# A decoder block whose TensorE queue is written by hand in the mixers: weaving order, new delays, an earlier second attention

## The chip, the cores and the metric

The kernel runs on one core of one Trainium2 chip. The metric is the device time of one execution in microseconds (us). Three runs of the kernel before gave 2710.49 us in the median, from 2708.99 to 2712.02. A program on this core drives five engines that run side by side: TensorE (PE) multiplies matrices, VectorE (DVE) and ScalarE (ACT) work elementwise, GpSimd (POOL) does a few small things, and SyncE (SP) issues the transfers (DMA). Each engine works off its own queue in the order in which the program was built; an instruction whose operands are not there holds up everything behind it on that engine.

## What is computed

One layer of a decoder block over 2048 tokens of width 1024, all in float32. The reference, cut to its skeleton:

```python
h = modulate(rms_norm(x, g_pre_mix), shift_m, scale_m)
proj = h @ w_in                      # attn q|k|v, mLSTM q|k|v|o, i|f gates, branch gates A|B
y_a = sliding_window_attention(rope(q_a), rope(k_a), v_a, sinks)     # 8 heads, 2 kv heads, window 128
q_m, k_m = silu(causal_depthwise_conv(q_m, k_m))
h_m = mlstm_chunkwise(q_m, k_m, v_m, i_pre, f_pre)                   # 4 heads of 128
y_m = sigmoid(o_m) * head_layer_norm(h_m)
merged = sigmoid(g_a) * (y_a @ w_branch_attn) + sigmoid(g_m) * (y_m @ w_branch_mlstm)
x = x + gate_m * rms_norm(merged @ w_out, g_post_mix)
h2 = modulate(rms_norm(x, g_pre_ffn), shift_f, scale_f)
x = x + gate_f * rms_norm((silu(h2 @ w_gate) * (h2 @ w_up)) @ w_down, g_post_ffn)
```

Every large product is made of three TensorE products of a high and a low part of each operand (`mm3`), so that the rounding of one part is made good by the other.

## The kernel before

**Stages.** The sequence is cut into two superblocks of 1024 tokens, each of two blocks of 512 (b0 and b1), each of four tiles of 128. A superblock (line 736 on) goes through the mixers: first the attention's queries (q) and keys and values with the gates' pre-activations (kv) of b0, then the mLSTM values (`vm`) of b0, then kv, q and `vm` of b1, then fourteen pairs of the projections that both blocks share (`in_pair`, line 1168; products of seven parts each that stand for eight), then the two output products of each block (`outputs`). After both superblocks comes the feed-forward part (`phase2`), which the change does not touch.

**Weaving.** The large products are a list of parts that `run2` goes through one by one. Everything else is a *stream*: a generator that emits a few instructions and then yields a delay. A virtual clock `now` counts the TensorE time emitted so far (`mm`, line 204, adds 0.422 ns per column of a two-part product, at least 110 ns; `transpose`, line 209, adds 110 ns). After each few products `tick` runs the streams whose delay is over. So a stream's delay says how much TensorE work is to lie between one of its steps and the next. The streams are

- `hprep` (line 486): eight steps that transpose the normalised input of a block, scale it on ACT and take its low part on DVE; for b1 each pair of steps is followed by four subtractions (lines 534 to 537) that build the sums T1 to T4 for the shared products;
- `hsums` (line 540): a transfer within the on-chip memory and eight casts and subtractions (lines 551 and 552) that split two of these sums;
- `q_stream` and `k_stream` (lines 764 and 791): after the rotary embedding (`rope`, lines 757 to 761, on DVE), TensorE transposes, and the result is stored to DRAM;
- `gates` (line 832): the scans of the mLSTM gates;
- `attention` (line 895), two at a time (`attention_stream`, streams 0 and 1 take every other tile): load, 24 score products, maximum on DVE, exponentials on ACT (line 946), a product on POOL (line 950), 16 transposes, four products with the values (PV), evacuation and store;
- `mlstm`, with `chunk_state` and `chunk_out` for each of eight tiles, and `conv` for the convolution.

**What sets the order.** `build` opens the program with a scheduler that simulates the engines (`schedule_with_timeline_sim=True`): on each engine it places next what its simulation finds ready. So in the kernel before, the order in which the program emits instructions, and with it every delay, is only a proposal. On all five engines the queue is what the scheduler made of it.

**Pools.** PSUM has four banks for the large products (`acc`) and four for all streams (`mix`). Split weights have four tiles, raw weights two.

Of the kernel before, what the change touches and what calls it, by code (L numbers as in the profile page):

```python
# [24 lines left out]
NT = TB // P  # L25
# [3 lines left out]
T2 = 1024  # L29
# [6 lines left out]
NEG = -1.0e30  # L36


L_X, L_HT, L_HS = 16000.0, 1400.0, 1500.0
L_ROPE, L_ROPEK, L_QK, L_ATT2 = 5000.0, 2100.0, 1500.0, 3500.0  # L40
L_GATE, L_SCAN = 1800.0, 3000.0
L_SOFT, L_PT, L_PV = 8000.0, 1300.0, 1000.0
L_ML, L_KW, L_OUT, L_STATE = 3200.0, 2600.0, 1500.0, 1500.0
L_S, L_LN = 1800.0, 5000.0
L_LOAD, L_HP2, L_HC = 5000.0, 1000.0, 3000.0
L_TANH, L_CONV, L_HD = 1500.0, 4000.0, 5000.0
L_REST = (2000.0, 1800.0, 2500.0, 2500.0)

# [23 lines left out]
def decoder_block(ctx: ExitStack, tc: tile.TileContext, a: dict, out: bass.AP, dbg=None):  # L72
# [124 lines left out]
    now = [0.0]  # L197
# [13 lines left out]
    def spawn(gen, delay=0.0):  # L211
        st = [now[0] + delay, gen, False]
        streams.append(st)
        return st
# [15 lines left out]
    def finish(sts):  # L230
        for st in sts:
            while not st[2]:
                now[0] = max(now[0], min(q[0] for q in streams))
                tick()
# [251 lines left out]
    def hprep(b, first=False):  # L486

        odd = b % 2
        xs = []
        xbs = x_first if first else [load_x(x_d[b * TB:(b + 1) * TB, :], big, i) for i in range(2)]  # L490
        V_NAMES = ("T3", "T2") if odd else ("T1", "T4")
        for n in V_NAMES:
            HR[n] = big([4, TB])
        vs = [HR[n] for n in V_NAMES]
        for i in range(2):
            xb = xbs[i]
            ss = small.tile([P, 4], F32, tag="ss", name=nm("ss"), bufs=4)
            for t in range(2):
                for hf in range(2):
                    A.activation(vs[i][:, 2 * t + hf, :], xb[:, t, hf * 512:(hf + 1) * 512], AF.Square,  # L500
                                 accum_out=ss[:, 2 * hf + t:2 * hf + t + 1])
            V.tensor_tensor(ss[:, 0:2], ss[:, 0:2], ss[:, 2:4], op=ALU.add)
            r = rsqrt_of_sumsq(ss[:, 0:2], 2)
            for t in range(2):
                if first:
                    A.activation(xb[:, t, :], xb[:, t, :], AF.Copy, scale=r[:, t:t + 1])
                else:
                    V.tensor_scalar(xb[:, t, :], xb[:, t, :], r[:, t:t + 1], None, op0=ALU.mult)
                xs.append(xb[:, t, :])
        yield L_X  # L510

        def one(k):
            name = f"{k // 4 + 1}{odd + 1}"
            hi, lo = (hc_part(name, i)[:, k % 4, :] for i in range(2))
            ps = mix_tile()
            for t in range(NT):
                transpose(ps[:, t * P:(t + 1) * P], xs[t][:, k * P:(k + 1) * P])
            A.activation(hi, ps, AF.Identity, scale=s1[:, k:k + 1], bias=sh1[:, k:k + 1])  # L518
            v = vs[k // 4][:, k % 4, :]
            A.activation(v, ps, AF.Identity, scale=s1[:, k:k + 1], bias=sh1[:, k:k + 1])  # L520
            (G if first else V).tensor_tensor(lo, v, hi.bitcast(F32), op=ALU.subtract)

        if not odd:
            for k in range(KD):
                one(k)
                yield L_HT
            return
        for k in range(4):
            one(k)
            yield L_HT  # L530
            one(k + 4)
            yield L_HT
            t1, t2, t3, t4 = (HR[n][:, k, :] for n in ("T1", "T2", "T3", "T4"))
            V.tensor_tensor(t1, t3, t1, op=ALU.subtract)
            V.tensor_tensor(t3, t2, t3, op=ALU.subtract)
            V.tensor_tensor(t2, t2, t1, op=ALU.subtract)
            V.tensor_tensor(t4, t4, t2, op=ALU.subtract)
            yield L_HT

    def hsums(names):  # L540

# [194 lines left out]
    def superblock(sb):  # L736
# [158 lines left out]
        def attention(n):  # L895
# [71 lines left out]
            for src_, u, st_, sp_ in ((pfs, int(first), True, first), (pcs, 1, False, True)):  # L967
                for g, p_ in enumerate(src_):
                    mm(yps[g * 64:(g + 1) * 64, :], vat[:, u, g * 64:(g + 1) * 64], p_.rearrange("p j q -> p (j q)"), st_, sp_)
            now[0] -= 1500.0  # L970
            yh, yl = tm([P, 512], F32R), tm([P, 512], F32R)
            A.copy(yh, yps)
            V.tensor_tensor(yl, yps, yh.bitcast(F32), op=ALU.subtract)
# [5 lines left out]
        def attention_stream(u):  # L979
            for i in range(u, 2 * NT, 2):  # L980
                while i >= ready[0]:
                    yield 1000.0
                yield from attention(b0 * NT + i)
                done_att[0] += 1
                yield 500.0
# [1 line left out]
        done_att = [0]  # L987

        def attend(b):
            finish(R["qk"])  # L990
            ready[0] = (b - b0 + 1) * NT
            if b == b0:
                R["att"] = [spawn(attention_stream(0), L_QK), spawn(attention_stream(1), L_QK + L_ATT2)]
            R["gs", b] = [spawn(gates(b), L_QK)]

        def end_attention(n):
            while done_att[0] < n:
# [283 lines left out]
        yield start  # L1281
        for z in q_kv(b0):
            yield from z
        yield lambda: attend(b0)
        yield from vm(b0)
        yield lambda: finish([hps[b1]])
        yield lambda: hps.update(t=spawn(hsums(("T2", "T4"))))
        q1, kv1 = (list(z) for z in q_kv(b1))
        yield from kv1
        yield from q1  # L1290
        yield from vm(b1)

        def start_f():
            finish([hps["t"]])
            HC.pop("12")
            hps["t"] = spawn(hsums(("T1", "T3")))
            attend(b1)

        yield start_f
        pairs = [("om", 0), ("qk", 0), ("om", 1), ("qk", 1), ("ga", 0), ("qk", 2), ("ga", 1), ("qk", 3),  # L1300
# [1 line left out]
        for i, (kind, p) in enumerate(pairs):  # L1302
            parts = list(in_pair(kind, p))
            if sb == 0 and i == 4:
                yield lambda: R.update(ada_m=[spawn(ada_stream([(2, "gate")], 6000.0))])
            if i == 0:
                yield from parts[:3]
                yield lambda: finish([hps["t"]])
                parts = parts[3:]
            if i + 1 == len(pairs):  # L1310
                yield from parts[:2]
                yield lambda: end_attention(NT)
                yield lambda: (load_y(b0, 0), load_g(b0, 0))
                parts = parts[2:]
            yield from parts
            if (kind, p) == ("qk", 3):
                yield lambda: finish(convs + R["gs", b0] + R["gs", b1])
                yield lambda: spawn(mlstm(), L_ML)
# [4 lines left out]
    hps = {}  # L1323
# [485 lines left out]
    def open_ffn():  # L1809
        p1.close()  # L1810
        F["pool"] = ctx.enter_context(tc.tile_pool(name="fpool", bufs=1, reuse_waits="tile"))

    def program():
        for i, ch in enumerate(ADA):
            if i == 3:
                yield lambda: tables.update({0: rope_tables(0)})
            yield lambda ch=ch: first_h(*ch)
        items = [it for sb in range(NSB) for it in superblock(sb)]
        last = max(i for i, it in enumerate(items) if isinstance(it, Part))
        yield from items[:last]  # L1820
        yield lambda: next(phase2)
        yield from items[last:]

# [46 lines left out]
```

## Time and profile before

| | |
|---|---|
| runs, median (lowest to highest) | 2710.49 us (2708.99 to 2712.02) |
| the profiled execution | 2716.59 us |
| its span in the profile | 2714.9 us |
| mean granted TensorE clock | 0.99 |
| first superblock's mixers | about 50 to 683 us |
| second superblock's mixers | about 683 to 1420 us |
| feed-forward part | about 1420 to 2715 us |
| largest transfer groups | weights of the input projection, 48 of 1024 KB; 154 stores of 256 KB |

A profile shows one execution. Busy time of an engine is given per stretch of the span; the granted clock is the share of the full TensorE clock that the throttle let through; "idle before" an instruction is put down to what released it. Matmuls overlap: a product of 512 columns is listed with some 0.39 us, while in a dense stretch one starts every 0.23 us. So whether TensorE is held up is read from its idle time, its clock and the number of products in a stretch together.

### The profile page before, as it was taken

To read this page: it belongs to the slowest core of one execution; us is meant where nothing else is said; L and a number is where in the kernel's file an instruction comes from. 1 tells how busy PE (TensorE), PEld (TensorE's weight loads), DVE (VectorE), ACT (ScalarE), POOL (GpSimd) and SP (SyncE) were. 2 spreads that over 40 slices of the span, in tenths; PEclk is the share of its full clock that TensorE was granted. 3 is DMA by queue.
4 is the path that set the end of the run, shared out by engine and by line. 5 is a ranking of instruction groups with operands and counts; after the bars stand their busy time and mean duration, and the time that the engine had idled before them with its cause. 6 is when DMAs were issued, how large, how long until landed. Compare 5 with 4: busy or idle time off the path is not lost.

```text
span 2714.9 us, 35793 instructions
## 1 busy us (share of the span) xinstructions
PE 2639.2 (97%) x12310; PEld 2138.9 (79%) x12310; DVE 1986.2 (73%) x3906; ACT 1299.8 (48%) x2558; POOL 148.2 (5%) x189
## 2 busy tenths in 40 slices
PE   6989999999998999999999999999999999999998
PEld 4867788888885678888887888888877888888886
DVE  7968788778695778876687777776677676766456
ACT  5556544444755564444563443335554333333444
POOL 2010001100101000110000000000000000000000
PEclk8999999999998999999999999999999999999999
DMA  7654355897574544678765564436675232324566
GB/s 249 206 184 157 128 172 179 269 340 248 196 235 147 196 138 138 213 231 291 251 224 198 175 201 152 155 113 213 215 271 188 97 117 86 113 97 144 186 210 217
DMA packets 353639, 511.90 MB, mean 189 GB/s; under 512 B 25120, under 2 KB 213660, under 8 KB 348208
## 3 DMA queue, kind: packets, MB, share of 16 engines
q1 hardware_dynamic: 353456, 509.61, 56.9%
q8 instruction: 97, 1.59, 0.2%
q14 instruction: 86, 0.70, 0.1%
HBM read 357.12 MB, written 144.02 MB: 185 GB/s over the span
## 4 chain that ended last, share of the span: by engine, by line
PE 85%; DVE 7%; DMA 4%; ACT 2%; issue 1%; POOL 0%; SPq 0%; DVEq 0%; ACTq 0%; POOLq 0%
PE acc L204 61%; PE mix L204 22%; PE mix L209 2%; DVE hl L1357 1%; DVE tm L428 1%; DMA raw<-as_d 1%; ACT tm L946 1%; ACT hl L1356 1%; DMA raw<-in_w_in_dram 1%; DMA at_d<-tx 0%; DMA big<-in_x_dram 0%; DVE wlo L260 0%; DMA tx<-in_w_ada_dram 0%; DVE w L1667 0%; DMA at<-at_d 0%
## 5 line engine op out<-in xcount | busy, mean ns | idle before, releaser
L204 PE MATMUL acc<-big,hl 128*128 128x512 f32 x3936 | 940.8, 394 | 4.3 <-ACT tx L827 1.8
L204 PEld LDWEIGHTS acc<-big,hl 128*128 128x128 f32 x3936 | 733.3, 188 | 172.5 <-issue 13.8
L1356 ACT CAST hl<-raw 128x512 fp32r<-128x512 f32 x732 | 440.1, 621 | 493.4 <-PE acc L204 222.2
L1357 DVE TENSOR_TENSOR hl<-raw,hl 128x512 fp32r<-128x512 f32 x732 | 496.3, 694 | 194.8 <-ACT hl L1356 194.0
L204 PE MATMUL acc<-whi,big 128*128 128x512 f32 (+1 forms) x1280 | 379.3, 377 | 10.8 <-ACT big L518 8.4
L204 PEld LDWEIGHTS acc<-whi,big 128*128 128x128 f32 x1280 | 236.2, 192 | 52.4 <-ACT big L518 8.5
L204 PE MATMUL mix<-big,hl 128*128 128x512 f32 x1056 | 263.9, 391 | 1.7 <-ACT hl L1356 1.1
L204 PE MATMUL acc<-wlo,big 128*128 128x512 f32 (+1 forms) x640 | 241.2, 379 | 6.4 <-DVE wlo L260 6.4
L204 PE MATMUL acc<-hl,hl 128*128 128x512 f32 x1008 | 237.4, 393 | 5.1 <-DVE hl L1357 3.4
L204 PEld LDWEIGHTS mix<-big,hl 128*128 128x128 f32 x1056 | 197.9, 188 | 45.9 <-ACT hl L1356 1.9
L204 PEld LDWEIGHTS acc<-hl,hl 128*128 128x128 f32 x1008 | 187.0, 188 | 50.9 <-DVE hl L1357 8.8
L204 PE MATMUL mix<-hl,hl 128*128 128x512 f32 x792 | 182.7, 391 | 1.3 <-DVE hl L1357 0.9
L204 PEld LDWEIGHTS mix<-hl,hl 128*128 128x128 f32 x792 | 147.9, 188 | 35.3 <-DVE hl L1357 3.1
L204 PE MATMUL acc<-big,whi 128*128 128x512 f32 x512 | 157.4, 393 | 0.0
L260 DVE TENSOR_TENSOR wlo<-raw,whi 128x1024 fp32r<-128x1024 f32 (+1 forms) x96 | 109.0, 1137 | 65.5 <-ACT whi L259 59.8
L259 ACT CAST whi<-raw 128x1024 fp32r<-128x1024 f32 (+1 forms) x96 | 94.3, 983 | 123.8 <-PE acc L204 110.4
L204 PEld LDWEIGHTS acc<-wlo,big 128*128 128x128 f32 x640 | 123.7, 193 | 28.3 <-DVE wlo L260 8.6
L475 POOL TENSOR_TENSOR rs<-ms,nhalf 128x1 f32<-128x1 f32 (+1 forms) x56 | 42.6, 772 | 1617.5 <-DVE ms L473 1610.5
L204 PE MATMUL mix<-hcT4h,hl 128*128 128x512 f32 x352 | 117.7, 395 | 0.7 <-ACT hl L1356 0.7
L204 PE MATMUL acc<-hcT2h,hl 128*128 128x512 f32 x352 | 117.6, 394 | 0.0
L204 PEld LDWEIGHTS acc<-big,whi 128*128 128x128 f32 x512 | 95.4, 188 | 19.2
L204 PE MATMUL acc<-big,wlo 128*128 128x512 f32 x256 | 97.7, 393 | 0.0
(330 smaller groups left out, 3491.5 us busy)
## 6 DMA issues: line engine op xcount, KB each, us to landing
raw<-in_w_in_dram SPq DMA_DIRECT2D x48, 1024.0 KB
as_d<-w SPq DMA_DIRECT2D x154, 256.0 KB
raw<-as_d SPq DMA_DIRECT2D x70, 512.0 KB
raw<-in_w_ffn_gate_dram SPq DMA_DIRECT2D x22, 1024.0 KB
raw<-in_w_ffn_up_dram SPq DMA_DIRECT2D x22, 1024.0 KB
raw<-ws_d SPq DMA_DIRECT2D x40, 512.0 KB
y_d<-tm SPq DMA_DIRECT2D x64, 256.0 KB
tx<-in_w_ada_dram SPq DMA_DIRECT2D x64, 256.0 KB
```

The source lines that it names most:

```text
L204: T.matmul(o, lhsT=lhsT, rhs=rhs, start=start, stop=stop, skip_group_check=resumed)
L209: T.transpose(o, i, ident[:k, :k])
L259: A.copy(hv, src)
L260: V.tensor_tensor(lv, src, hv.bitcast(F32), op=ALU.subtract)
L428: V.scalar_tensor_tensor(acc, raw[:, k, :], c_, acc, op0=ALU.mult, op1=ALU.add)
L475: G.tensor_tensor(r[:, :n], ms[:, :n], nhalf[:, :n], op=ALU.pow)
L946: A.activation(sc[g][:, j, :], sc[g][:, j, :], AF.Exp, bias=nm_[:, hd:hd + 1], accum_out=sums[:, hd:hd + 1])
L1356: A.copy(v(hi), src)
L1357: V.tensor_tensor(v(lo), src, v(hi).bitcast(F32), op=ALU.subtract)
```

## The change

TensorE's queue is taken out of the scheduler's hands: from the end of the first q product of the first superblock up to the last part of the mixers, a manual schedule for PE alone makes TensorE issue in the order in which the program emits. DVE, ACT, POOL and SP are still scheduled by simulation. Beside that

- nearly all delays are set anew, most of them longer (`L_SOFT` between scores and the first transposes 8 to 12 us, `L_PV` 1 to 3 us, `L_QK` 1.5 to 6 us, `L_ROPE` 5 to 7 us, `L_ROPEK` 2.1 to 3 us, `L_LN` 5 to 9 us), and a correction of the virtual clock by 1.5 us in `attention` is taken out;
- the four subtractions per step of b1's `hprep` get a stream of their own, `hcombos`, which is started after `vm` of b0 with a delay of 12 us and goes on with the sums T2 and T4; T1 and T3 are split by two streams instead of one, T3 later;
- `attend`, which opens a block's gates and attention, no longer drains the q and k streams at its place: it starts a stream that looks every 0.3 us whether they are done, waits `L_QK`, and then lets the attention of that block begin; for b1 it is called ahead of `vm` instead of behind it;
- the second attention stream looks for work every 4.5 us instead of every 1 us.

```diff
-L_ROPE, L_ROPEK, L_QK, L_ATT2 = 5000.0, 2100.0, 1500.0, 3500.0
-L_GATE, L_SCAN = 1800.0, 3000.0
-L_SOFT, L_PT, L_PV = 8000.0, 1300.0, 1000.0
-L_ML, L_KW, L_OUT, L_STATE = 3200.0, 2600.0, 1500.0, 1500.0
-L_S, L_LN = 1800.0, 5000.0
-L_LOAD, L_HP2, L_HC = 5000.0, 1000.0, 3000.0
+L_X, L_HT, L_HS, L_HCB = 16000.0, 1400.0, 1500.0, 12000.0
+L_ROPE, L_ROPEK, L_QK, L_ATT2 = 7000.0, 3000.0, 6000.0, 7000.0
+L_GATE, L_SCAN = 6000.0, 9000.0
+L_SOFT, L_PT, L_PV = 12000.0, 1500.0, 3000.0
+L_ML, L_KW, L_OUT, L_STATE = 3200.0, 3500.0, 1500.0, 1500.0
+L_S, L_LN = 2500.0, 9000.0
+L_LOAD, L_HP2, L_HC = 7000.0, 1000.0, 3000.0
...
+    def hcombos():
+        for k in range(4):
             t1, t2, t3, t4 = (HR[n][:, k, :] for n in ("T1", "T2", "T3", "T4"))
             V.tensor_tensor(t1, t3, t1, op=ALU.subtract)
             V.tensor_tensor(t3, t2, t3, op=ALU.subtract)
+            yield L_HS
             V.tensor_tensor(t2, t2, t1, op=ALU.subtract)
             V.tensor_tensor(t4, t4, t2, op=ALU.subtract)
-            yield L_HT
+            yield L_HS
+        yield from hsums(("T2", "T4"))
...
-            now[0] -= 1500.0
...
                 while i >= ready[0]:
-                    yield 1000.0
+                    yield 1000.0 + 3500.0 * u
...
         def attend(b):
-            finish(R["qk"])
-            ready[0] = (b - b0 + 1) * NT
+            def stream():
+                while not all(st[2] for st in R["qk"]):
+                    yield 300.0
+                yield L_QK
+                ready[0] = (b - b0 + 1) * NT
+                yield from gates(b)
+            R["gs", b] = [spawn(stream())]
             if b == b0:
                 R["att"] = [spawn(attention_stream(0), L_QK), spawn(attention_stream(1), L_QK + L_ATT2)]
-            R["gs", b] = [spawn(gates(b), L_QK)]
...
         for z in q_kv(b0):
             yield from z
+            if sb == 0 and not pe_order:
+                pe_order.append(0)
+                yield lambda: order.enter_context(tc.manual_schedule(engines={mybir.EngineType.PE}))
...
-        yield lambda: hps.update(t=spawn(hsums(("T2", "T4"))))
+        yield lambda: hps.update(t=spawn(hcombos(), L_HCB))
...
         yield from q1
+        yield lambda: attend(b1)
         yield from vm(b1)
...
-            hps["t"] = spawn(hsums(("T1", "T3")))
-            attend(b1)
+            hps["t"] = spawn(hsums(("T1",)))
+            hps["t3"] = spawn(hsums(("T3",)), L_HD)
...
-                yield from parts[:3]
+                yield from parts[:4]
                 yield lambda: finish([hps["t"]])
-                parts = parts[3:]
+                yield parts[4]
+                yield lambda: finish([hps["t3"]])
+                parts = parts[5:]
...
         yield from items[:last]
+        yield order.close
         yield lambda: next(phase2)
```

No product, elementwise instruction or transfer is added or taken away: the same products, transposes, casts, subtractions and transfers are issued, in another order.

More of the change, by code (lines that the diff above doesn't have):

```diff
@@ L36 @@
 NEG = -1.0e30
-L_X, L_HT, L_HS = 16000.0, 1400.0, 1500.0
-L_ROPE, L_ROPEK, L_QK, L_ATT2 = 5000.0, 2100.0, 1500.0, 3500.0
-L_GATE, L_SCAN = 1800.0, 3000.0
-L_SOFT, L_PT, L_PV = 8000.0, 1300.0, 1000.0
-L_ML, L_KW, L_OUT, L_STATE = 3200.0, 2600.0, 1500.0, 1500.0
-L_S, L_LN = 1800.0, 5000.0
-L_LOAD, L_HP2, L_HC = 5000.0, 1000.0, 3000.0
+L_X, L_HT, L_HS, L_HCB = 16000.0, 1400.0, 1500.0, 12000.0
[5 more added lines that the diff above has]
+L_LOAD, L_HP2, L_HC = 7000.0, 1000.0, 3000.0
 L_TANH, L_CONV, L_HD = 1500.0, 4000.0, 5000.0
@@ L1811, in open_ffn @@
         F["pool"] = ctx.enter_context(tc.tile_pool(name="fpool", bufs=1, reuse_waits="tile"))
+    pe_order, order = [], ExitStack()
     def program():
```

## The prediction

> **What bounds the kernel now.** I read the page's busy times first, then the stretches, then the waits and the timeline of the stretches that stand out.
>
> ```profile
> span 2714.9 us, 35793 instructions
> ...
> PE 2639.2 (97%) x12310; PEld 2138.9 (79%) x12310; DVE 1986.2 (73%) x3906; ACT 1299.8 (48%) x2558; POOL 148.2 (5%) x189
> ```
>
> TensorE is the bound, but a busy TensorE is not a dense one. The stretches below (PE, weight loads, DVE, ACT, POOL busy, granted clock, DMA share, GB/s) show where it is thin.
>
> ```profile
> core 0: us, PE busy (x) PEld busy (x) DVE busy (x) ACT busy (x) POOL busy (x), PEclk, DMA share, GB/s
> 66.00:108.00 42.00, 39.46 (x242) 34.61 (x241) 39.77 (x105) 27.01 (x46) 1.17 (x2) 1.00 0.56 171
> 155.00:186.00 31.00, 24.14 (x116) 12.52 (x114) 16.13 (x44) 16.64 (x56) 4.68 (x5) 0.89 0.46 143
> 206.00:312.00 106.00, 105.97 (x504) 76.33 (x504) 83.57 (x182) 67.31 (x173) 9.36 (x8) 1.00 0.41 132
> 312.00:683.00 371.00, 371.00 (x1796) 311.64 (x1795) 293.00 (x622) 177.18 (x317) 32.14 (x32) 1.00 0.71 235
> 403.00:570.00 167.00, 167.00 (x889) 143.00 (x889) 127.96 (x323) 77.31 (x150) 25.36 (x22) 1.00 0.76 243
> 741.00:783.00 42.00, 39.13 (x239) 34.32 (x238) 37.13 (x104) 21.94 (x36) 0.00 (x0) 1.00 0.60 184
> 838.00:868.00 30.00, 20.58 (x95) 11.12 (x92) 15.03 (x42) 15.81 (x55) 4.67 (x5) 0.72 0.37 116
> 1750.00:1800.00 50.00, 50.00 (x220) 40.97 (x219) 39.33 (x64) 18.10 (x33) 0.00 (x0) 1.00 0.43 139
> ```
>
> The last row is the feed-forward part: 220 products of 512 columns in 50 us, 0.227 us each. That is dense. In the mixers two stretches are not: 155 to 186 us (6.9 us idle, clock 0.89) and 838 to 868 us (9.4 us idle, clock 0.72). They are the third and fourth attention tile of each superblock's first block. And in two stretches DVE is all but full: 39.77 of 42 us and 37.13 of 42. They are the fronts of the superblocks, where the rotary embedding of q and k, the low parts of b1's input and the sums T1 to T4 meet. All else that the change reorders (206 to 312, and 312 to 683 with the mLSTM tiles at 403 to 570) has next to no idle time on TensorE, so there it can only lose.
>
> **Part 1: what TensorE's new order takes out.** In 838 to 868 us TensorE waits in turn for loads, DVE and POOL:
>
> ```profile
> PE mix L209 <- DVE tm L933: 4.1, 1, 4.1
> PE mix L204 <- DMA at<-at_d: 2.4, 1, 2.4
> PE mix L209 <- POOL tm L950: 1.6, 2, 0.9
> ```
>
> The reason is in the queue: the old order puts 4.0 and 5.3 us of TensorE work between the last scores of these tiles and their first PV product, since the scheduler laid scores, transposes and PV of both tiles back to back. (I count TensorE work through the two queues with 0.227 us per product of 512 columns, 0.12 for 264, 0.105 for a transpose, 0.115 for a score product, 0.87 for a PV product.) The chain that has to fit in:
>
> ```profile
> 841.08 2.74 PE L204 MATMUL mix<-at 64*128 64x256 f32 x24 [2.43 <-DMA at<-at_d]
> 845.10 2.93 PE L204 MATMUL mix<-at 64*128 64x256 f32 x24 [1.28 <-DVE tm L933]
> 846.63 1.28 ACT L946 ACT_TABLE_LOAD   x1 [2.18 <-DVE es L941]
> 850.25 1.04 POOL L950 TENSOR_TENSOR tm<-tm,sums 128x512 f32<-128x512 f32 x1 [25.52 <-DVE sums L949]
> 854.26 4.37 PE L204 MATMUL mix<-tm,at 128*64 128x512 f32 x8
> 858.22 1.04 POOL L950 TENSOR_TENSOR tm<-tm,sums 128x512 f32<-128x512 f32 x1 [5.06 <-DVE sums L949]
> 861.49 1.68 PE L204 MATMUL mix<-tm,at 128*64 128x512 f32 x2
> ```
>
> From the end of the scores (843.8 and 848.0) to the end of the first POOL product (851.3 and 859.3) it takes 7.5 and 11.2 us, to PV 10.4 and 13.5. The new order has 11.5 to 13.2 us between scores and first transposes for the sixteen tiles, and 16.8 to 20.3 to PV. So products of `vm` and kv cover the chain, with 4 us to spare for the first tile of a pair and half a microsecond for the second. What can come back: idle 6.86 + 9.42 = 16.3 us, and some 4 us of slow clock, 20 at most. I take 16, since the second tile's chain is not quite covered.
>
> On the clock the Trainium skill has a rule ("TensorE: Matmul & The Clock Gate", "Why this matters for your kernels"): idle gaps over about 3 us drop TensorE to half its clock until it has been busy for as long again. The granted 0.72 and 0.89 agree. By it each long wait that the new order makes costs up to 2 us more than the wait; the sum below would be some 5 us higher.
>
> **Part 2: what it puts in: the rotary embeddings of the fronts.** Here TensorE's transposes move the other way. Between the last product of the first q tile and the transpose of the last k tile the old order has 38.6 and 39.2 us of TensorE work (first and second superblock), the new one 21.1 and 24.9: `L_ROPE` and `L_ROPEK` count from each evacuation, and the transposes now stand where the program emits them, in front of the products of `vm` that used to cover them. DVE can't keep up:
>
> ```profile
> 68.29 0.42 DVE L757 TENSOR_TENSOR tx<-tx,sin 128x256 f32<-128x256 f32 x1
> 102.66 0.22 DVE L761 TENSOR_TENSOR tx<-tx,tx 128x64 f32<-128x64 f32 x1
> ...
> 743.03 0.42 DVE L757 TENSOR_TENSOR tx<-tx,sin 128x256 f32<-128x256 f32 x1
> 743.36 0.42 DVE L758 TENSOR_TENSOR tx<-tx,sin 128x256 f32<-128x256 f32 x1
> ...
> 744.37 0.68 DVE L536 TENSOR_TENSOR big<-big,big 128x512 f32<-128x512 f32 x1
> 744.97 0.70 DVE L260 TENSOR_TENSOR wlo<-raw,whi 128x528 fp32r<-128x528 f32 x1
> 745.59 0.69 DVE L759 TENSOR_TENSOR tx<-tx,cos 128x512 f32<-128x512 f32 x1
> ...
> 760.08 1.22 DVE L260 TENSOR_TENSOR wlo<-raw,whi 128x1024 fp32r<-128x1024 f32 x1
> ...
> 777.52 0.22 DVE L761 TENSOR_TENSOR tx<-tx,tx 128x64 f32<-128x64 f32 x1
> ```
>
> From the first q rotation to the last k rotation DVE takes 34.6 us (68.29 to 102.88) and 34.7 (743.03 to 777.74). TensorE did not feel it, because it came to the last k transpose only at 107.7 and 782.3:
>
> ```profile
> 107.71 0.27 PE L209 MATMUL mix<-ident,tx 128*128 128x128 f32 x1
> ...
> 782.34 0.27 PE L209 MATMUL mix<-ident,tx 128*128 128x128 f32 x1
> ```
>
> In the changed kernel's DVE queue the same stretch in the second superblock holds 16 rotations of half a tile at 0.335 us (start to start above) and 4 at 0.60, 36 subtractions of 128x512 at 0.60 (8 low parts, 16 sums T, 8 low parts of T2 and T4 that the scheduler pulled forward, 4 low parts of q), 3 split weights at 0.62 and 2 at 1.22, and 6.4 us of small ones: 40 us. The delay of `hcombos` doesn't keep its subtractions out, since it orders TensorE's queue alone. In the first superblock the queue has 33.1 us. With 0.6 us for ACT's copy ahead of it, TensorE is late by 33.1 + 0.6 - 21.1 = 12.6 and 40.0 + 0.6 - 24.9 = 15.7 us, 28 together. Behind the waiting transposes stand all products of `vm`, ready as they are. The old queue lost 42 - 39.46 = 2.5 and 42 - 39.13 = 2.9 us there, so 23 are new. What DVE did early it need not do later: I take back 5 us, for the eight pulled-forward subtractions. Net 18. The bounds: 5 if the scheduler's queue runs better than its sum, 28 if nothing comes back.
>
> **Part 3: the second block's attention and the rest.** The four tiles of b1 lie within 62 us of TensorE work (scores of the first to PV of the last), against 106 us in the row 206 to 312. DVE's queue holds 47 us for these 62, but 21 for the first 17.5. So 3 us of wait in each superblock, from 0 (the convolutions give way) to 8. That `attend` for b1 stands ahead of `vm` moves the first score by 1 us of TensorE work only: it still waits for the q streams and `L_QK`. Eight mLSTM tiles take 97 us of TensorE work instead of 145, and DVE's queue 85 us in them (88%), where the row 403 to 570 shows 127.96 of 167 (77%). The shortest distance there is scores to numerator, 2.1 us:
>
> ```profile
> 433.67 1.06 PE L204 MATMUL mix<-ld,ld 128*128 128x128 f32 x8
> 435.87 0.69 DVE L1051 TENSOR_TENSOR tm<-mix,tm 128x512 f32<-128x512 f32 x1
> ```
>
> That chain ended 1.8 us after the scores, so it fits where DVE is free at once and is late by one instruction (0.7 us) where not: 2.5 us for eight tiles. The old queue also let two products slip ahead at many part boundaries of the pairs, the new one doesn't; a cast of one evacuation (0.6 us) lies under a part of 12 x 0.227 = 2.7 us, so nothing, at worst 0.5 us at some 60 places in both superblocks. Loads have 7 instead of 5 us and cost nothing.
>
> **The sum.** -16 + 18 + 2 x 3 + 2 x 2.5 = +13 us against the profiled execution's 2716.6. That one lies 6.1 us above the median of the runs, 2710.5, so the forecast is 2723.5, rounded 2723.
>
> **The rivals.** *The fronts are covered (faster).* If DVE's wait in the fronts is no longer than the 5 us of before plus 5, because TensorE's other work there (ACT, raw weights) was late anyway, and b1 costs nothing, the sum is -16 + 5 + 5 = -6 to -11: 2702. For it: DVE was full in both fronts before (39.77 and 37.13 of 42), and TensorE lost under 3 us. Against: it lost little because of the 14 to 17 us of cover that are now gone.
>
> *Pair boundaries decide (much slower).* TensorE stops at each boundary where the old queue slipped, 60 places at 0.5 us, once DVE is over 88% full: +30, 2750. For it: the 88%. Against: in 312 to 683 us nothing waited.
>
> *It evens out.* The change doesn't make TensorE denser, it moves the wait from the third and fourth tile to the rotation, at equal price (16 against 16): 2710 within 5 us. For it: DVE's work is the same and it is the engine that both wait for.
>
> **How the numbers follow.** A measurement tells 0.2% (5.4 us) from no change. Forecast 0.42 (own range 2712 to 2740), covered fronts 0.29, boundaries 0.14, even 0.15. Slower by over 0.2% (above 2715.9): most of the forecast, all of the boundaries, 0.53; same 0.15; faster (below 2705.1) 0.32. The range goes from 2688 (nearly all of 20 us gained, the fronts covered) to 2752.
>
> **What would show it.** Right: in the changed kernel TensorE waits for DVE's key rotation (transposes out of tx) in both fronts, over 10 us each; no waits for POOL over 2 us at the third and fourth tile; clock near 1.00 there. Part 2 falls if the idle time of the fronts stays near 3 us. Part 3 falls if idle time appears at the pairs. Wrong altogether would be a wait that none of these stretches held, such as a transfer that SP, still in the scheduler's order, issues too late for TensorE's fixed one.

## The result, and the profile after

The changed kernel is slower: 2792.72 us in the median (2787.18 to 2793.43), against 2711.24 us for the kernel before in the same comparison, a ratio of 1.0294 [1.0278, 1.0309]. The profiled execution took 2792.43 us. The forecast was 2723, with a range up to 2752: the sign was right, the size was not.

The page after, its span and its busy times:

```profile
span 2790.7 us, 35799 instructions
...
PE 2642.5 (95%) x12310; PEld 2150.0 (77%) x12310; DVE 1992.1 (71%) x3906; ACT 1306.1 (47%) x2558; POOL 152.0 (5%) x189
```

The span grew by 75.8 us, TensorE's busy time by only 3.3 (2639.2 before). So some 72 us are idle time of TensorE, and the stretches say where. Rows of the changed kernel (PE, weight loads, DVE, ACT, POOL busy, clock, DMA share, GB/s). Its second superblock runs 23 us late in the front (the first rotation starts at 766.36 us, before at 743.03), so the rows of the kernel before that belong to it, in the second fence, are taken 23 us earlier. Further on the lag grows, and the rows hold somewhat different work; since the kernel before has only 3.4 us of idle time from 892 us to the end of its mixers, the differences of idle time stand all the same:

```profile
66.00:108.00 42.00, 30.99 (x184) 27.35 (x183) 40.67 (x106) 26.50 (x47) 0.79 (x2) 0.88 0.54 176
130.00:186.00 56.00, 46.55 (x268) 35.52 (x269) 30.29 (x117) 34.62 (x113) 8.85 (x9) 0.88 0.52 158
206.00:312.00 106.00, 97.18 (x479) 72.14 (x478) 78.96 (x171) 65.94 (x170) 8.84 (x8) 0.95 0.45 153
403.00:570.00 167.00, 155.54 (x827) 131.05 (x826) 127.11 (x325) 75.52 (x153) 26.27 (x22) 0.99 0.64 201
764.00:812.00 48.00, 32.47 (x194) 29.29 (x193) 41.52 (x105) 26.66 (x46) 0.00 (x0) 0.82 0.58 193
812.00:915.00 103.00, 89.38 (x476) 68.95 (x476) 62.73 (x189) 48.78 (x140) 9.69 (x9) 0.89 0.50 157
915.00:1010.00 95.00, 77.71 (x403) 58.24 (x402) 69.09 (x150) 52.27 (x145) 9.55 (x8) 0.91 0.55 182
1080.00:1250.00 170.00, 155.92 (x782) 130.04 (x781) 135.97 (x321) 73.84 (x149) 23.96 (x20) 0.97 0.54 167
```

```profile
130.00:186.00 56.00, 49.15 (x227) 31.75 (x226) 33.09 (x101) 32.99 (x108) 9.38 (x9) 0.94 0.43 130
741.00:789.00 48.00, 44.96 (x282) 39.65 (x280) 41.28 (x113) 23.81 (x40) 0.00 (x0) 1.00 0.66 214
789.00:892.00 103.00, 89.45 (x462) 65.72 (x460) 74.20 (x204) 53.16 (x147) 9.20 (x9) 0.90 0.58 191
892.00:987.00 95.00, 91.60 (x435) 68.57 (x435) 73.85 (x166) 62.59 (x166) 8.32 (x8) 0.98 0.50 156
1057.00:1227.00 170.00, 170.00 (x889) 144.78 (x889) 138.25 (x330) 76.95 (x153) 26.84 (x22) 1.00 0.68 211
```

The first two columns after the stretch are its length and TensorE's busy time; the difference is its idle time. Put beside the terms of the forecast, that gives (us):

| term of the forecast | forecast | idle time, before to after | change |
|---|---|---|---|
| fronts with the rotary embeddings (part 2) | +23, net +18 | 2.5 to 11.0 and 3.0 to 15.5 | +21 |
| attention of b0, third and fourth tiles (part 1) | -16 | 6.9 to 9.5 and 13.6 to 13.6 | +3 |
| attention of b1 (part 3) | +6 | 0.0 to 8.8 and 3.4 to 17.3 | +23 |
| mLSTM (part 3) | +5 | 0 to 11.5 and 0 to 14.1 | +26 |

What TensorE waited for in the mixers (us in total, times, longest):

```profile
PE mix L209 <- DVE tx L766: 24.0, 8, 5.4
PE mix L204 <- issue: 14.2, 4, 5.9
PE acc L204 <- ACT tx L832: 12.0, 3, 8.0
PE mix L204 <- DVE tm L938: 9.6, 5, 3.1
PE acc L204 <- ACT tx L1511: 7.0, 2, 4.1
PE mix L204 <- DVE tm L857: 6.7, 2, 4.3
PE mix L204 <- DVE tm L1027: 5.0, 5, 2.0
```

Only the first line was in the forecast with a size near this (L766 is the last step of the rotation, line 761 before; line numbers are those of the changed kernel from here on). The second and the last belong together: the state products of the mLSTM, whose weighted keys DVE makes in line 1027 ("issue" says that the profile names no releaser; the rows below show what came just before). The third is a bank of the large products that isn't evacuated. This is what two of these waits look like in time. First the longest one; ACT's queue around it:

```profile
127.67 1.28 ACT L951 ACT_TABLE_LOAD   x1
...
130.25 0.40 ACT L951 ACTIVATE tm<-tm,nmx 128x128 f32<-128x128 f32 x1 [1.31 <-DVE nmx L945]
...
136.62 0.23 ACT L894 ACTIVATE ex<-ex 128x48 f32<-128x48 f32 x1
136.75 0.56 ACT L832 COPY tx<-acc 128x512 f32<-128x512 f32 x1
```

The second row is the first of sixteen exponentials of two attention tiles (line 951), 0.4 us apart; the third comes behind the last of them. The copy that frees a bank of `vm` stands behind them; TensorE's last product began at 129.10 and it waited 8.0 us. The scores of both tiles had been issued 3 us apart (at 118.3 and 121.0), as the program weaves them. Then the mLSTM; DVE, POOL and TensorE:

```profile
443.58 0.60 PE L209 MATMUL mix<-ident,ld 128*128 128x128 f32 x4
443.93 3.69 PE L204 MATMUL acc<-big,hl 128*128 128x512 f32 x15
...
445.83 0.75 DVE L428 SCALAR_TENSOR_TENSOR tm<-tx,c_sb,tm 128x512 f32<-128x512 f32 x1 [2.89 <-DMA tx<-in_w_ada_dram]
...
449.14 1.40 POOL L1086 TENSOR_TENSOR cf<-vr,nhalf 128x4 f32<-128x4 f32 x1 [12.91 <-DVE vr L1084]
...
450.57 1.00 DVE L1087 TENSOR_TENSOR cf<-cf,den 128x4 f32<-128x4 f32 x1 [0.91 <-POOL cf L1086]
...
452.77 0.67 DVE L1027 TENSOR_TENSOR tm<-mix,ex 128x512 f32<-128x512 f32 x1
...
453.55 2.06 PE L204 MATMUL mix<-vmt,tm 128*128 128x129 f32 x8 [5.93 <-issue]
```

The keys are transposed at 444.2. The instruction that weights them takes 0.67 us, but comes 8.6 us later, since the normalisation of the tile before, splits and evacuations of the large products, a term of the conditioning stream (`ada_stream`) and a power on POOL stand in front of it in DVE's queue. Part of it DVE stands idle itself: until 445.83 for the load of that term, and 0.9 us for POOL. TensorE had 3.8 us of other work placed between.

### The profile page after: what moved, and what is told of

Read it like the earlier page. It is cut to its first block, busy times and chain, and to the rows that moved or that the text cites. A ratio compares the mean times of both kernels' runs of the same rounds, so it can differ in the third digit from the quotient of the medians.

```text
span 2790.7 us, 35799 instructions
## 1 busy us (share of the span) xinstructions
PE 2642.5 (95%) x12310; PEld 2150.0 (77%) x12310; DVE 1992.1 (71%) x3906; ACT 1306.1 (47%) x2558; POOL 152.0 (5%) x189
## 4 chain that ended last, share of the span: by engine, by line
PE 78%; DVE 9%; DMA 6%; ACT 4%; issue 3%; POOL 0%; SPq 0%; DVEq 0%; POOLq 0%; ACTq 0%
PE acc L204 56%; PE mix L204 21%; PE mix L209 2%; DVE hl L1371 1%; ACT tm L951 1%; DMA tx<-in_w_ada_dram 1%; DVE tm L428 1%; ACT hl L1370 1%; DMA at_d<-tx 1%; DMA big<-big 1%; DMA raw<-as_d 1%; DMA at<-at_d 1%; DVE tm L938 0%; DVE big L557 0%; DMA ld<-qk_d 0%
## 5 line engine op out<-in xcount | busy, mean ns | idle before, releaser
L204 PE MATMUL acc<-whi,big 128*128 128x512 f32 (+1 forms) x1280 | 401.2, 387 | 21.1 <-ACT tx L832 12.0
L204 PEld LDWEIGHTS acc<-whi,big 128*128 128x128 f32 x1280 | 245.1, 198 | 68.3 <-ACT tx L832 12.7
L475 POOL TENSOR_TENSOR rs<-ms,nhalf 128x1 f32<-128x1 f32 (+1 forms) x56 | 45.1, 817 | 1713.4 <-DVE ms L473 1709.7
```

Source lines behind the costliest of these rows:

```text
L204: T.matmul(o, lhsT=lhsT, rhs=rhs, start=start, stop=stop, skip_group_check=resumed)
L475: G.tensor_tensor(r[:, :n], ms[:, :n], nhalf[:, :n], op=ALU.pow)
```

## The experiments

Base is the changed kernel where nothing else is said, and each run is the median of its comparison with the kernel before (2711 to 2713 us in each). First: is it the fixed queue, or what else was edited?

**TensorE scheduled, all other edits kept.**

```diff
-                yield lambda: order.enter_context(tc.manual_schedule(engines={mybir.EngineType.PE}))
+                yield lambda: None
```

> The changed kernel with all its edits but the manual schedule: TensorE is placed by the scheduler again. Theory (the fixed queue is the cause: TensorE stands at waits that the scheduler's order steps round): the 60 to 80 us go, and since the scheduler now lays 18 to 30 us between scores and PV of all sixteen tiles (4.0 and 5.3 before at the third and fourth), the idle 16 us of before at those tiles go too: 2690 to 2712. Rival (the new delays, the early attention of b1 and the split of the sums are the cause): at least 2750.

2698.58 us, 0.9949 [0.9935, 0.9964]: the theory. The fixed queue costs 94 us, and without it the change is a gain of about 0.5%. This version beats both kernels. Its rows for the attention of b0 show most of the idle time gone that part 1 was after:

```profile
130.00:186.00 56.00, 53.10 (x276) 41.40 (x276) 39.94 (x127) 32.12 (x92) 6.58 (x6) 0.96 0.58 178
789.00:892.00 103.00, 96.28 (x532) 73.19 (x531) 82.22 (x220) 57.98 (x158) 9.58 (x9) 0.98 0.68 226
```

Idle 2.9 and 6.7 us, where the kernel before had 6.9 and 13.6.

**The kernel before with the manual schedule alone.**

```diff
         for z in q_kv(b0):
             yield from z
+            if sb == 0 and not pe_order:
+                pe_order.append(0)
+                yield lambda: order.enter_context(tc.manual_schedule(engines={mybir.EngineType.PE}))
...
         yield from items[:last]
+        yield order.close
```

> The kernel before with the manual schedule alone, delays and streams as they were. Theory (fixed queue; the longer delays of the change soften it): TensorE has 0.2 to 2.8 us of work between a k tile's evacuation and its transposes (3.5 to 4.5 in the changed kernel) and 10.5 to 13 from scores to PV (17 to 20), so every such wait is longer: 2830 to 2900. Rival (new delays and early attention cause the loss): 2710 to 2750.

2887.47 us, 1.0651: the theory. With the old, shorter delays the fixed queue costs 174 us, against 94 with the change's delays and stream edits. These two together are a remedy for the fixed queue that doesn't go far enough; which of them does how much of it by hand was not run.

**Longer rotary delays.**

```diff
-L_ROPE, L_ROPEK, L_QK, L_ATT2 = 7000.0, 3000.0, 6000.0, 7000.0
+L_ROPE, L_ROPEK, L_QK, L_ATT2 = 16000.0, 12000.0, 6000.0, 7000.0
```

> The changed kernel with L_ROPE 16 and L_ROPEK 12 us instead of 7 and 3: TensorE has 13 us of work between a k tile's evacuation and its transpose, and 17 for q. Theory of the prediction's second part (the rotary transposes come too early for DVE): the 24.0 us that TensorE waits for the rotations in the profile, less up to 6 us that come back at the sums behind, go: 2765 to 2778. Rival (DVE is short in the fronts as a whole, and TensorE then waits for the next DVE result): within 8 us of 2793.

2760.14 us: 32.6 us less, more than expected. The waits for L766 fell from 24.0 to 2.0 us, and those for the evacuation of `vm` (line 832) with them, from 12.0 to 0.8. New ones came: 11.8 us for the copy of line 811, which wants a `tx` tile.

```profile
PE acc L204 <- ACT tx L811: 11.8, 7, 4.6
PE mix L209 <- DVE tx L766: 2.0, 1, 2.0
PE acc L204 <- ACT tx L832: 0.8, 1, 0.8
```

So the gain is not that of the fronts alone. In the first front (66 to 108 us) TensorE idles 14.4 us, more than the 11.0 of the changed kernel: there the rival has a point. In the second (764 to 812 us) it idles 7.7 instead of 15.5, and in b0's attention (130 to 186 and 812 to 915 us) 6.7 and 8.4 instead of 9.5 and 13.6.

**The evacuations of vm on DVE.**

```diff
-                A.copy(v, ps)
+                V.tensor_copy(v, ps)
```

> The changed kernel with the evacuations of vm on DVE instead of ACT (16 copies of 128x512). Theory (vm's products wait 12.0 us, 8.0 at the longest, because the copy that frees their accumulation bank stands in ACT's queue behind the exponentials of two attention tiles): these waits go, 2780 to 2786. Rival (DVE is the shorter queue: 16 x 0.68 = 11 us more on it delay rotations and masks by as much): 2790 to 2805.

2792.42 us: the rival. The 8.0 us wait is gone (in 130 to 206 us TensorE idles 4.9 instead of 9.5 us), and elsewhere DVE's masks (L938, from 9.6 to 11.8 us) and the loads of attention tiles (from 2.0 to 5.1) take it back. A wait removed at one place is not yet time gained.

**Longer distance from key transposes to state products.**

```diff
-L_ML, L_KW, L_OUT, L_STATE = 3200.0, 3500.0, 1500.0, 1500.0
+L_ML, L_KW, L_OUT, L_STATE = 3200.0, 9000.0, 1500.0, 1500.0
```

> The changed kernel with L_KW 9 us instead of 3.5: TensorE has 10 us of work between the key transposes of an mLSTM tile and the state products that need DVE's weighted keys, instead of 3.8. Theory (the mLSTM stretches lose because these products come too early for DVE; waits of 14.2 and 5.0 us stand against them): 2773 to 2780. Rival (DVE itself stands still in these stretches, on the loads of w_ada and on POOL's powers, so that the wait goes to the next product): 2786 to 2796.

2761.44 us, 31.3 less; more than the 19 us of listed waits. In the mLSTM stretches (403 to 570 and 1060 to 1250 us) TensorE idles 3.1 us in all, where it idled 25.5; where the rest of the 31.3 comes from was not followed up. In 403 to 570 us the only wait left on TensorE's list is one of another kind:

```profile
PE mix L209 <- DMA ld<-qk_d: 1.1, 1, 1.1
```

**b1's attention behind its values.**

```diff
-        yield lambda: attend(b1)
         yield from vm(b1)
+        yield lambda: attend(b1)
```

> The changed kernel with b1's attention called behind its values instead of ahead of them: the first scores of b1 move back by 13.6 us of TensorE work in both superblocks (counted through the queues); distances inside each attention tile stay. Theory (the early call lays scores, gate scans and the rotary work of b1 upon each other, which is what 206 to 312 and 880 to 1000 us pay, 8.8 and 14.9 us more idle time than before): 2778 to 2786. Rival (the waits hang on the distances inside each chain, not on the place): 2789 to 2797.

2783.35 us, 9.4 less: within the theory's range.

**The stream edits alone, scheduled, with all delays of before.**

```diff
-                yield lambda: order.enter_context(tc.manual_schedule(engines={mybir.EngineType.PE}))
+                yield lambda: None
...
-L_SOFT, L_PT, L_PV = 12000.0, 1500.0, 3000.0
-L_ML, L_KW, L_OUT, L_STATE = 3200.0, 3500.0, 1500.0, 1500.0
+L_SOFT, L_PT, L_PV = 8000.0, 1300.0, 1000.0
+L_ML, L_KW, L_OUT, L_STATE = 3200.0, 2600.0, 1500.0, 1500.0
...
```

> The kernel of the run without the manual schedule, with the delays of the kernel before: the edits of the streams alone, TensorE scheduled. Counted through the queue, the third and fourth attention tiles again have 5.1 and 5.3 us from scores to PV. Theory (the 12 to 14 us that the scheduled version wins come from the longer delays, which the scheduler follows at these tiles): 2708 to 2716. Rival (the stream edits win them): 2694 to 2703.

2712.09 us, 1.0001 [0.9992, 1.0011]: the theory. In the attention TensorE waits for POOL again, 11.7 us in all (`PE mix L209 <- POOL tm L955`), a wait that the scheduled version with the new delays does not list. So the stream edits are worth nothing by themselves, and the new delays 13.5 us under the scheduler.

**The sums T on POOL** (`V` becomes `G` in all four subtractions of `hcombos`).

```diff
-            V.tensor_tensor(t1, t3, t1, op=ALU.subtract)
+            G.tensor_tensor(t1, t3, t1, op=ALU.subtract)
...
```

> The changed kernel with the sixteen subtractions of the sums T per superblock on POOL instead of DVE (about 16 x 0.68 = 11 us off DVE). Theory of the prediction's second part (DVE's queue in the fronts is overfull, and these subtractions, pulled forward, stand ahead of rotations): TensorE's 24.0 us of waits for rotations shrink by a third to a half, 2780 to 2785. Rival (they fill gaps of DVE's queue): 2788 to 2796.

2797.27 us, 4.6 above the changed kernel, which is within the spread of the two comparisons and a little beyond the rival's range. The gain of the theory did not come, but the run doesn't decide between the two, since DVE was not relieved. Why is in the last section.

**The three delays together.**

```diff
-L_ROPE, L_ROPEK, L_QK, L_ATT2 = 7000.0, 3000.0, 6000.0, 7000.0
+L_ROPE, L_ROPEK, L_QK, L_ATT2 = 16000.0, 12000.0, 6000.0, 7000.0
-L_ML, L_KW, L_OUT, L_STATE = 3200.0, 3500.0, 1500.0, 1500.0
+L_ML, L_KW, L_OUT, L_STATE = 3200.0, 9000.0, 1500.0, 1500.0
...
-        yield lambda: attend(b1)
         yield from vm(b1)
+        yield lambda: attend(b1)
```

> The changed kernel, TensorE's queue by hand, with three edits together: L_ROPE 16 and L_ROPEK 12, L_KW 9, b1's attention called behind its values. Each alone took 32.6, 31.3 and 9.4 us off 2792.7. Theory (separate waits in separate stretches): they add, 2717 to 2726, still not below the scheduled version's 2698.6. Rival (each wait gone uncovers the next one, since DVE is the engine behind all of them): 2735 to 2755.

2745.78 us: the rival; 73 us alone, 47 together. Part of the reason is a tile. This is the front of that kernel, ACT, DVE and TensorE:

```profile
106.35 0.23 DVE L762 TENSOR_TENSOR tx<-tx,sin 128x64 f32<-128x64 f32 x1 [1.32 <-DMA at_d<-tx]
...
107.17 0.38 ACT L811 COPY tx<-acc 128x264 f32<-128x264 f32 x1 [3.44 <-DMA at_d<-tx]
...
107.61 0.50 PE L204 MATMUL acc<-whi,big 128*128 128x512 f32 x1 [2.17 <-ACT tx L811]
```

A q tile and a kv tile each hold two of the nine `tx` tiles until their stores are done. With 16 and 12 us of delay they are held so long that ACT cannot copy kv out, the bank stays full, and TensorE waits (12.2 us in all for line 811).

**The same, scheduled.**

```diff
-                yield lambda: order.enter_context(tc.manual_schedule(engines={mybir.EngineType.PE}))
+                yield lambda: None
```

> The same three edits with TensorE scheduled. Theory (the scheduler steps round these waits whatever the delays, and only the place of the attention tiles moves its queue): 2695 to 2703, the 2698.6 of the scheduled version within 0.2%. Rival (longer delays help there too): below 2692.

2705.93 us, 0.9975 [0.9962, 0.9987]: the rival falls, the theory's range is missed by 3 us, and it is 7 us above the scheduled version with the change's own delays. Longer isn't better there.

**By hand only in the mLSTM stretches.**

```diff
-                yield lambda: order.enter_context(tc.manual_schedule(engines={mybir.EngineType.PE}))
+                yield lambda: None
...
-                yield lambda: spawn(mlstm(), L_ML)
+                yield lambda: (order.enter_context(tc.manual_schedule(engines={mybir.EngineType.PE})), spawn(mlstm(), L_ML))
+        yield order.close
         yield from outputs(b0)
```

> The changed kernel with TensorE scheduled in the fronts and by hand only from the start of the mLSTM stream to the end of the pairs in each superblock. Theory (the mLSTM stretches lose 25 to 31 us by themselves, because DVE's weighted keys come later than 3.8 us of TensorE work): 2698.6 + 25 to 31 = 2723 to 2730. Rival (DVE is late there because the fronts by hand pushed its work back): 2698 to 2706.

2744.33 us: 45.7 us above the scheduled version, more than the theory's 31 (and far from the rival), with the fronts scheduled. The same wait of 5.9 us as in the changed kernel stands there. DVE is not late because of the fronts.

**More time for the loads of w_ada.**

```diff
-                    yield gap
+                    yield 2.5 * gap
                     ada_terms(acc, raw, k, 1)
```

> The changed kernel with 2.5 times the gap between a load of w_ada and DVE's use of it. Theory (the two long waits of 5.9 and 4.7 us in the mLSTM stretches come from DVE standing 2.9 and 3.3 us on such a load, with the weighted keys behind it in its queue): these waits shrink to 2 us, 2780 to 2786. Rival (the keys are late by their own distance): 2788 to 2797.

2802.18 us: the gain didn't come, and the time is above the rival's range too. The wait at the same products is still 5.7 us long. The longer stream also ends in a wait of its own (17.3 us for line 466). In the first superblock the edit didn't reach what it aimed at, since DVE still stands at such a load just ahead:

```profile
442.08 0.75 DVE L428 SCALAR_TENSOR_TENSOR tm<-tx,c_sb,tm 128x512 f32<-128x512 f32 x1 [3.30 <-DMA tx<-in_w_ada_dram]
```

In the second (1080 to 1250 us) it did: DVE waits for these loads 1.3 instead of 3.3 us, and TensorE waits for its state products as long as before (10.7 us with lines "issue" and L1027, after 10.6). So there the theory falls; in the first it was not tested.

**L_KW 9 and the late call, rotary delays as in the change.**

```diff
-L_ML, L_KW, L_OUT, L_STATE = 3200.0, 3500.0, 1500.0, 1500.0
+L_ML, L_KW, L_OUT, L_STATE = 3200.0, 9000.0, 1500.0, 1500.0
...
-        yield lambda: attend(b1)
         yield from vm(b1)
+        yield lambda: attend(b1)
```

> The changed kernel with L_KW 9 and b1's attention called late; the rotary delays stay at 7 and 3. Theory (these two act in separate stretches and add: 2792.7 - 31.3 - 9.4): 2747 to 2756; then the long rotary delays are worth only some 6 us on top of them (2745.8 with all three). Rival (they already take part of the same waits): 2758 to 2765.

2761.38 us: the rival. On top of L_KW the late call is worth nothing.

**The same, with L_ROPE 9 and L_ROPEK 7.**

```diff
-L_ROPE, L_ROPEK, L_QK, L_ATT2 = 7000.0, 3000.0, 6000.0, 7000.0
+L_ROPE, L_ROPEK, L_QK, L_ATT2 = 9000.0, 7000.0, 6000.0, 7000.0
```

> As the run before this one, with L_ROPE 9 and L_ROPEK 7 (16 and 12 in the run with all three). Theory (16 and 12 us hold the nine tx tiles, so that the evacuations of kv wait for a store of q and TensorE for their accumulation bank, 12.2 us; in between neither the rotation nor the tile is late): 2725 to 2738. Rival (DVE is short behind all of them): 2743 to 2752.

2730.60 us, 1.0067 [1.0052, 1.0082]: the theory. Line 811 is all but gone from the waits (0.2 us). 62 of the 82 us are won back with the queue still by hand. The rotary delays are worth 30.8 us in this place: against the run before, the waits for L766 fall from 21.6 to 10.0 us and those for the evacuation of `vm` from 11.8 to nothing. The largest that are left are these 10.0 us, 9.6 for loads of attention tiles and 8.5 for masks.

**The same, with 3 us between the halves of a tile's scores.**

```diff
                 if jj == 0:
-                    yield 0
+                    yield 3000.0
```

> As the run before this one, with 3 us of TensorE work put between the two halves of an attention tile's scores. Theory (the scores take all four mix banks, so whatever stream comes next waits for DVE's masked copies that free them; such waits add up to 6 to 14 us in every run by hand): 6 to 12 us less than the run before. Rival (the wait only moves by three microseconds of work): within 4 us of it.

2751.97 us: a miss for both, 21 us slower. The waits for masks stay (7.5 us after 8.5), and waits for POOL's products grow from 4.6 to 14.4 us, the longest 7.5; line 811 is back with 8.0 us. (The profiled execution, 2760.83 us, is the longest of the four.) In the first pair of tiles the scores end later (at 121.3 and 125.9 us, where they ended at 119.0 and 122.3), and POOL's first product starts 3.2 us later (135.91 against 132.73). Why that costs 21 us is open.

**By hand only in the mLSTM stretches, with L_KW 9.**

```diff
-L_ML, L_KW, L_OUT, L_STATE = 3200.0, 3500.0, 1500.0, 1500.0
+L_ML, L_KW, L_OUT, L_STATE = 3200.0, 9000.0, 1500.0, 1500.0
```

> TensorE by hand from the start of the mLSTM stream to the end of the pairs only, with L_KW 9 instead of 3.5. Theory (of the 45.7 us which that cost, nearly all hang on the 3.8 us between key transposes and state products): 2700 to 2712. Rival (the fixed queue loses at many other places there, the boundaries of the pairs among them): 2720 to 2735.

2714.25 us, 1.0012 [1.0002, 1.0022]: just above the theory's range. Of 45.7 us, 30.1 hang on this one distance. Of the other 15.7, TensorE's list shows 6.8 as waits for one evacuation (line 1512), 3.1 us in each of the stretches in which the section by hand is opened.

**The attention's delays alone, scheduled, in the kernel before.**

```diff
-L_SOFT, L_PT, L_PV = 8000.0, 1300.0, 1000.0
+L_SOFT, L_PT, L_PV = 12000.0, 1500.0, 3000.0
...
-            now[0] -= 1500.0
```

> The kernel before, TensorE scheduled, with L_SOFT 12, L_PT 1.5 and L_PV 3 us and without the 1.5 us correction of the clock: nothing else. In its queue the third and fourth tiles of the superblocks have 5.3 and 13.0, and 7.1 and 13.9 us from scores to PV, instead of 4.0 and 5.3. Theory (the gain of the scheduled version is these tiles' chains of 10.4 and 13.5 us, covered by work): most of the second tiles' waits go, 2699 to 2706. Rival (the other delays win it, by bringing these tiles up earlier): 2708 to 2714.

2707.35 us, 0.9989 [0.9978, 1.0]: between the two, nearer the rival. These delays alone are worth between nothing and 6 us of the 13.5; which of the others bring the rest is open.

## Why the prediction was wrong

**What bounds it.** That TensorE's order can only lose where it had no idle time was right: most of the loss is in stretches that were full before. The terms add up to +13 in the forecast and to +73 in the rows. Of the 60 us between them part 1 holds 19, b1's attention 17, the mLSTM 21 and the fronts 3.

**Part 1, -16: not returned.** The chain of the third and fourth tiles was covered as forecast; the waits for POOL there are gone (0.4 us are left in all the mixers). But the forecast looked at POOL, DVE and the loads, and not at ACT: `vm`'s products, which were to be the cover, wait for their own evacuation behind exponentials of attention tiles. In the first superblock that is 8.0 of the 9.5 us of idle time; in the second it is 4.1 of 13.6, and masks (4.2), splits of weights (3.5) and a last rotation (1.7) make up most of the rest. The idle time stayed (6.9 to 9.5, 13.6 to 13.6), and the clock, forecast near 1.00, is 0.88 and 0.89. That such a gain exists is shown by the scheduled version: 2.9 and 6.7 us idle in these stretches, and 0.5% less time than before.

**Part 2, +18: right in kind, and near in size.** The fronts' idle time grew by 21 us against 23 new ones forecast; TensorE stands at these transposes in the second front:

```profile
804.50 0.30 PE L209 MATMUL mix<-ident,tx 128*128 128x128 f32 x1 [1.46 <-DVE tx L766]
809.99 0.48 PE L209 MATMUL mix<-ident,tx 128*128 128x128 f32 x1 [5.19 <-DVE tx L766]
```

The rotations took 45.1 us there (766.36 to 811.50) against 40.0 counted. Of "over 10 us each" for the wait only the second front holds (17.2 us); the first has 6.8. Whether the 5 us taken back came back can't be told: the longer rotary delays won 31 to 33 us, but some 12 of the waits that they took away are those for the evacuation of `vm`, which the forecast put at nothing. Whether the sums in DVE's queue delayed the rotations stays open too: on POOL they held up DVE just as long.

**Part 3, +11: the step that failed most.** For the mLSTM the forecast took "the shortest distance there", scores to numerator, found its own chain 1.8 us long, and charged one instruction per tile: 5 us. What decides is another distance, key transposes to state products, and not by the length of its chain (0.67 us) but by DVE's queue in front of it (8.6 us). A longer distance is worth 31.3 us in the changed kernel and 30.1 with only this part by hand, 22 of the 31.3 as idle time in the mLSTM stretches, which had grown by 26. For b1's attention 23 us came instead of 6. That the early call "moves the first score by 1 us" compared it with the old queue; with the queue by hand it is 13.6 us. Its worth, though, was 9.4 us alone and nothing beside a longer L_KW, so the rest of b1's loss hangs on other waits: with all that was won (the run of 2730.60 us), TensorE still idles 7.5 us in 206 to 312 and 12.3 us in 880 to 1000, on masks, loads, POOL and evacuations. That rest stays open.

**The rivals.** Covered fronts and the even outcome are out. That pair boundaries decide is out: in the changed kernel the pairs run by hand, without mLSTM work beside them, through these two stretches, and TensorE has no idle time there:

```profile
312.00:403.00 91.00, 91.00 (x402) 74.99 (x400) 79.08 (x141) 42.30 (x70) 0.00 (x0) 1.00 0.47 148
1000.00:1080.00 80.00, 80.00 (x356) 63.41 (x355) 66.37 (x120) 40.72 (x69) 0.00 (x0) 1.00 0.46 142
```

The pairs among the mLSTM tiles cost at most 15.7 us over the scheduled version once L_KW is long, and some 7 of these are waits for one evacuation. The rival's idea that a busy DVE cannot keep a fixed order was nearer the truth than the forecast, though DVE was busy for 76 and 80% of the mLSTM stretches, not 88: it was the order in its queue that made it late.

**The clock.** By the Trainium skill's rule ("TensorE: Matmul & The Clock Gate", "Why this matters for your kernels") the sum was to be some 5 us higher. The granted clock did fall in the fronts and the attention, to 0.82 in the lowest of the rows; behind the wait of 8.0 us it is 0.50 from 135 to 140 us and 1.00 again from 145 us on. TensorE's busy time rose by 3.3 us in all. So the trace agrees with the half clock and, roughly, with the 5 us, and the slow clock is a small part of the 76.

**What the sum missed as a whole** is that it took the terms as separate. They are not: three edits that win 73 us alone win 47 together, and longer rotary delays also end waits for the evacuation of `vm`. The likely reason, argued from the rows and not tried by itself: all chains go through one DVE and one ACT, whose order the scheduler's simulation sets; a fixed TensorE queue turns each delay into a deadline for them, and stands at the first that is missed, with ready products behind it. Counted through the queues as in the forecast, the scheduled version has 18 to 36 us of TensorE work between scores and PV, the changed kernel 17 to 20.

## What to carry to other kernels

When one engine's queue is fixed and the others are not, price each distance by everything that stands in the producer's queue ahead of the result (8.6 us here), not by the result's own chain (0.67 us), and look at every engine in the loop, the evacuation of the covering work among them. A delay has two ends: too short and the engine stands at the result, too long and tiles are held that others need (rotary delays of 16 and 12 us lost 15 us against 9 and 7). Try a set of new delays with the scheduler left on before taking its order away: here the delays were worth 0.5%, and the order by hand cost 3.5%.

## What the runs showed of the hardware

The subtractions that were moved to POOL held up DVE one for one. In the run with the sums T on POOL, first DVE, then POOL:

```profile
92.00 1.32 DVE L763 TENSOR_TENSOR tx<-tx,sin 128x64 f32<-128x64 f32 x1
93.24 1.36 DVE L815 TENSOR_TENSOR tx<-tx,v_last 128x128 f32<-128x128 f32 x1
94.53 1.21 DVE L817 TENSOR_TENSOR gt<-tx,b_if 128x4 f32<-128x4 f32 x1
...
104.24 0.21 DVE L763 TENSOR_TENSOR tx<-tx,sin 128x64 f32<-128x64 f32 x1
```

```profile
91.96 1.28 POOL L538 TENSOR_TENSOR big<-big,big 128x512 f32<-128x512 f32 x1
93.20 1.26 POOL L541 TENSOR_TENSOR big<-big,big 128x512 f32<-128x512 f32 x1
94.42 1.31 POOL L537 TENSOR_TENSOR big<-big,big 128x512 f32<-128x512 f32 x1
```

A rotation of 64 columns takes 0.21 us when POOL is idle (104.24) and 1.32 us while POOL subtracts, an addition of four columns 1.21 us: in these microseconds DVE does one instruction for each of POOL's, in step with it. So the 11 us taken off DVE freed next to nothing: in 50 to 130 us it was busy for 63.9 us with 138 instructions, after 64.9 us with 166 in the changed kernel, and the longest wait for a rotation grew from 5.4 to 11.1 us. The Trainium skill ("SBUF — State Buffer", "SBUF: two separate sides") says that a DVE instruction with two inputs in SBUF, the on-chip memory, and a GpSimd instruction that reads SBUF lock each other out for a whole instruction; the 1.32 us beside POOL's 1.28 agree.
